# The remainder of a down projection as a fourth chunk of block products, with a rearranged end, an earlier weight split and another queue for the constants

## The chip, the core and the metric

The kernel runs on one core of one Trainium2 chip. A core has a matrix engine (TensorE, PE in the profile), a vector engine (VectorE, DVE), a scalar engine (ScalarE, ACT), a fourth general engine (GpSimd, POOL) and one that here only issues transfers (SyncE, SP). Transfers are also issued by ScalarE. Each engine works through its own list of instructions in order and waits on semaphores for the others. The metric is the device time of one execution in microseconds (us), the median of several runs.

## The reference

One encoder block on x of 1 x 1024 positions x 1024 channels, in float32; the last two steps are the ones at issue:

```python
h = rmsnorm(x, norm_mix_g[l])
z = jnp.einsum("bsd,de->bse", h, w_in[l])
... # short gated convolution; long convolution with layer norm
x = x + jnp.einsum("bse,ed->bsd", y, w_out[l])
h = rmsnorm(x, norm_ffn_g[l])
g = dwconv(jnp.einsum("bsd,df->bsf", h, w_gate[l]), conv_ffn_w[l])
v = jnp.einsum("bsd,df->bsf", h, w_up[l])
x = x + jnp.einsum("bsf,fd->bsd", jax.nn.silu(g) * v, w_down[l])
return rmsnorm(x, norm_final_g)
```

The inner width of the last part (F) is 2816, which is 22 tiles of 128. `w_down` maps these 22 tiles to 8 output tiles of 128 channels; each has 1024 positions, handled as two halves h of 512.

## The kernel before, in words

Channels lie on the 128 partitions, positions along the free axis. Every float32 product is made of three matmuls on a high and a low part of each operand (high x high, high x low, low x high), each 128 x 128 by 128 x 512. `split` makes the two parts: ScalarE copies to the high part (`whi`, `r`, `ahi`), VectorE subtracts it from the original to get the low part (`wlo`, `r`, `alo`; L93). GpSimd makes the first sums of weights (`s`, L511).

Wherever weights and operand can be cut into 2 x 2 blocks, a class `Pair` forms the product with seven block products instead of eight: m1 = A11 B11, m2 = A12 B21, m6 = S2 T2, m7 = S3 T3, m4 = A22 T4, m5 = S1 T1, m3 = S4 B22. S1 to S4 are sums of weight blocks, T1 to T4 sums of operand blocks. m1, m6, m7 and m4 accumulate in one PSUM bank (`a`), m2 in `b`, m5 and m3 in `c`; after each the running sum is taken where an output needs it. For the gate and up projections the two rows of blocks are the gate weights and the up weights of one F tile (`Ffn`, one gate/up pair per F tile); for the down projection they are two output tiles 2dp and 2dp + 1 (`Down`), and the columns are pairs of F tiles. There, half 0 of the even output tile is finished by m2, half 0 of the odd one by m4, half 1 of the odd one by m5 and m7, and half 1 of the even one by m3.

The program runs through these stages: first norm and in projection; the convolutions; out projection; second norm; gate/up, with 22 F tiles, the first ones handled apart ("plain", `NHEAD` = 2) while the operands of the block form are still being built; then the down projection. Each finished pair of F tiles 2q and 2q + 1 (pair q) goes to device memory in seven blocks (B11, T2, B21, T3, T1, T4, B22; `yd`, 256 KB each), four of which are differences made by GpSimd (L90). The down projection reads them back chunk by chunk: `NCH` = 3 chunks of `PPC` = 3 pairs, for each of four output pairs dp seven products of 3 x 3 = 9 matmuls. Two output pairs that work together are a couple. The last `NTAIL` = 4 F tiles are left over: they are stored whole (`ytail`, 512 KB each) and multiplied plainly, 12 matmuls for each of 8 tiles and 2 halves (`tail_mm`), first all of h = 0, then all of h = 1. After each, `done` adds it to the residual (VectorE), squares it (ScalarE) and adds the square to `accs[h]` (VectorE); `scale` multiplies the output by the norm's weight (ScalarE). When h = 0 is through, TensorE sums `accs[0]` over the partitions with a matrix of ones (`total3`), ScalarE takes the root (L1067), VectorE the reciprocal (L1069), and GpSimd multiplies the eight h = 0 outputs (`fin`, L1037), which SyncE stores, while TensorE works at h = 1. The last tile of h = 1 is finished in three pieces of 192, 192 and 128 positions, the multiplications shared between VectorE (5) and GpSimd (3).

TensorE's order is that of the program text (`manual_schedule`); in the last stage that of all four compute engines is. Elsewhere a scheduler sets the order of the other engines by its own costs, with `urgent` work ahead. SyncE's queue takes nearly all loads and stores in order; a store that waits for its data holds up all loads behind it.

## Time and profile before

| what | value |
|---|---|
| median of 3 runs | 1000.53 us (1000.17 to 1000.76) |
| the profiled execution, its own time | 1000.93 us |
| its span in the trace | 999.1 us |
| mean granted TensorE clock | 0.993 |
| matmul records | 4208 |
| transferred | 112.56 MB |

Times in rows of the trace count from the start of the span. A row of a timeline is: start, duration, engine, source line, operation, output <- input, shape, how many in a row, and in brackets the idle time before it and what ended it. A row of waits is: the engine and line that waited, what it waited for, us in total, how often, the longest. A row of windows is: from:to, its length, and the busy time of PE, weight load, DVE, ACT and POOL with the number of instructions, the granted clock, the busy share of the transfer engines and GB/s. A row of groups ends in count | busy us, mean ns | idle before. L93 and the like are lines of the kernel before.

### The profile page before, as it was taken

Reading aid. Unit: us, or ns where it says so; the run is one execution under the profiler, and the core shown is the slowest. Engines: PE = TensorE matmul, PEld = TensorE weight load, DVE = VectorE, ACT = ScalarE, POOL = GpSimd, SP = SyncE. Lnnn points to the kernel's source line nnn. Section 1 sums busy time; section 2 is a strip of 40 time slices with the busy share of each in tenths; the row PEclk is TensorE's granted clock in tenths of the full one; section 3 lists DMA queues with packets and bytes.
Section 4 is the critical chain, followed back from the end, with each engine's and each line's share of the span. In section 5 each row is a group of like instructions: output and inputs, shape, how many; then the busy total and the mean of one; then the engine's idle time right before and its main releaser. Section 6 shows DMA issues by size and latency. Waiting matters only on the chain.

```text
span 999.1 us, 11602 instructions
## 1 busy us (share of the span) xinstructions
PE 967.5 (97%) x4208; PEld 790.8 (79%) x4208; DVE 755.6 (76%) x888; ACT 452.8 (45%) x632; POOL 477.0 (48%) x303
## 2 busy tenths in 40 slices
...
GB/s 257 85 44 63 43 45 61 42 64 106 193 190 153 76 0 158 64 148 106 64 145 108 64 124 129 64 101 141 70 287 130 220 207 96 194 127 109 61 1 169
DMA packets 63274, 112.56 MB, mean 113 GB/s; under 512 B 5488, under 2 KB 27120, under 8 KB 62960
## 3 DMA queue, kind: packets, MB, share of 16 engines
...
q14 instruction: 25, 0.20, 0.1%
...
## 4 chain that ended last, share of the span: by engine, by line
PE 81%; DVE 9%; ACT 3%; issue 2%; DMA 1%; POOL 1%; POOLq 0%; SPq 0%; DVEq 0%; ACTq 0%
PE a L557 30%; PE mm L166 20%; PE c L557 15%; PE b L557 7%; DVE r L93 2%; PE c L692 1%; PE a L692 1%; PE mm L153 1%; PE mm L152 1%; PE mm L154 1%; PE y L154 1%; PE y L152 1%; PE y L153 1%; DMA raw<-wgate 1%; ACT whi L131 1%
## 5 line engine op out<-in xcount | busy, mean ns | idle before, releaser
L166 PE MATMUL mm<-r,whi 128*128 128x512 f32 x576 | 155.8, 389 | 0.0
L557 PE MATMUL a<-r,whi 128*128 128x512 f32 x472 | 145.7, 390 | 0.4 <-ACT a L542 0.4
L323 DVE SCALAR_TENSOR_TENSOR cv<-u,cst,cv 128x512 f32<-128x512 f32 x203 | 138.9, 751 | 1.7 <-ACT cv L317 1.2
L511 POOL TENSOR_TENSOR s<-raw,s 128x512 f32<-128x512 f32 (+1 forms) x31 | 57.5, 1854 | 161.5 <-DVE wlo L93 161.5
L166 PEld LDWEIGHTS mm<-r,whi 128*128 128x128 f32 x576 | 108.1, 188 | 22.6
L557 PE MATMUL c<-r,whi 128*128 128x512 f32 x392 | 121.1, 390 | 0.0
L93 POOL TENSOR_TENSOR wlo<-raw,whi 128x1024 fp32r<-128x1024 f32 x30 | 77.5, 2586 | 88.0 <-ACT whi L131 88.0
L131 ACT ACTIVATE whi<-raw 128x1024 fp32r<-128x1024 f32 (+1 forms) x68 | 69.2, 1020 | 103.5 <-PE mm L166 32.0
L557 PEld LDWEIGHTS a<-r,whi 128*128 128x128 f32 x472 | 88.4, 188 | 19.7 <-ACT a L542 0.8
L511 POOL TENSOR_TENSOR s<-up 128x512 f32<-128x512 f32 (+1 forms) x31 | 42.0, 1354 | 116.7 <-DMA up<-wup 96.8
L557 PE MATMUL a<-r,wlo 128*128 128x512 f32 x236 | 92.2, 391 | 2.8 <-DVE wlo L93 2.8
L166 PE MATMUL mm<-r,wlo 128*128 128x512 f32 x288 | 90.0, 389 | 0.0
L557 PEld LDWEIGHTS c<-r,whi 128*128 128x128 f32 x392 | 73.8, 188 | 16.0
L542 ACT ACTIVATE a<-a 128x512 f32<-128x512 f32 x80 | 47.5, 595 | 66.9 <-PE a L557 64.2
L131 ACT ACTIVATE whi<-s 128x1024 fp32r<-128x1024 f32 (+1 forms) x52 | 52.5, 1010 | 53.5 <-PE c L557 39.8
L557 PE MATMUL c<-r,wlo 128*128 128x512 f32 x196 | 76.5, 390 | 0.0
L635 DVE TENSOR_TENSOR t<-a,c 128x512 f32<-128x512 f32 x40 | 27.5, 687 | 64.4 <-ACT a L542 38.1
L557 PE MATMUL a<-r,ahi 128*128 128x512 f32 x224 | 70.5, 396 | 1.4 <-ACT a L542 1.4
L557 PE MATMUL b<-r,whi 128*128 128x512 f32 x232 | 71.4, 389 | 0.0
L93 DVE TENSOR_TENSOR wlo<-s,whi 128x1024 fp32r<-128x1024 f32 (+1 forms) x52 | 64.2, 1236 | 5.8 <-ACT whi L131 5.7
L131 ACT ACTIVATE r<-r 128x512 fp32r<-128x512 f32 x71 | 43.8, 628 | 49.8 <-DMA r<-ydB 23.3
L166 PEld LDWEIGHTS mm<-r,wlo 128*128 128x128 f32 x288 | 54.1, 188 | 11.2
(214 smaller groups left out, 2142.0 us busy)
## 6 DMA issues: line engine op xcount, KB each, us to landing
...
```

The lines of the kernel that those rows point to most:

```text
L93: eng.tensor_tensor(out=out, in0=a, in1=b, op=ALU.subtract)
L131: nc.scalar.activation(hi, y, AF.Copy)
L152: nc.tensor.matmul(out, whi, hi, start=first, stop=False)
L153: nc.tensor.matmul(out, whi, lo, start=False, stop=False)
L154: nc.tensor.matmul(out, wlo, hi, start=False, stop=last)
L166: nc.tensor.matmul(outs[h], w, a[h][z], start=s0, stop=s1)
L323: nc.vector.scalar_tensor_tensor(fin if k == KC - 1 else acc, src, w, acc, ALU.mult, ALU.add)
L511: self.eng.tensor_tensor(out=self.t[:, i * self.w : (i + 1) * self.w], in0=a, in1=b, op=op)
L542: nc.scalar.activation(t, b, AF.Copy)
L557: nc.tensor.matmul(out, w[wz][:, k, :], x[xz], start=first and k + wz + xz == 0, stop=k == n - 1 and wz == 1, skip_group_check=not first)
L635: nc.vector.tensor_tensor(out=out, in0=a, in1=b, op=op)
L692: nc.tensor.matmul(out, w[wz][:, k, :], xz, start=first and k == 0 and wz == 0 and xz is hi, stop=not first and k == 3 and wz == 1)
```

## The change

Four things change together.

The tail becomes a fourth chunk of the block form, with `NPL` = 2 pairs (9 and 10): 6 matmuls per product, seven products, four output pairs. The four left-over F tiles go to `yd` like the others: per pair three blocks straight and four differences from GpSimd. The last chunk's order is its own: m1, m6, m2, m7 and m4 of all four output pairs come first (m5 of the first two lies among them), so that h = 0 is complete; then the total of h = 0, now two accumulated products with ones since the last square does not go through `accs[0]`; then m5 and m3 for h = 1. In the last stage the additions of squares of h = 1 are on GpSimd (five, ahead of its eight multiplications), and VectorE multiplies all eight outputs of the first two pieces. An additional activation (Sqrt on one column, `warm`) is written before the last two m4 products. In SyncE's queue the store of the last h = 0 output pair stands behind two piece stores, with eight piece stores behind it.

In chunk 0, the sum after m5 of the first two output pairs goes through a ScalarE copy and a GpSimd addition instead of a VectorE addition.

The gate weights of F tile 3 (the fourth gate/up pair) are loaded and split before the second sums of F tile 2, into a place that the third pair's weights leave.

The constants are loaded as the first transfer of SyncE's queue instead of the first of ScalarE's.

```diff
-NTAIL = NF - 2 * NCH * PPC
+NPL = NF // 2 - NCH * PPC
...
     cuts = ((0, 2), (2, 4), (4, 8))
+    nc.sync.dma_start(cst, consts)
     nc.sync.dma_start(xs[0][:, 0, :], xT[0, :, 0])
-    nc.scalar.dma_start(cst, consts)
     load_w01(*cuts[0])
...
-    yd = {o: dpool.tile([P, NCH * PPC, H], F32, name=f"yd{o}") for o in OPS}
-    ytail = dpool.tile([NTAIL, P, S], F32, name="ytail")
+    yd = {o: dpool.tile([P, NF // 2, H], F32, name=f"yd{o}") for o in OPS}
...
-        if f >= NF - NTAIL:
-            nc.sync.dma_start(ytail[f - (NF - NTAIL)], cc)
-            return
...
-    def ff_prep(f):
-        raw, hl = g_job(f)
+    def ff_prep(f, job=None):
+        raw, hl = job or g_job(f)
...
         with urgent():
             to_op("T2", 0, 0)
+        job = g_job(NHEAD + 1)
         p2.w.update(s2.second(g2[0], up2))
         plain[1].second_b()
...
-            ff_prep(f + 1)
+            ff_prep(f + 1, job if f == NHEAD else None)
...
+    def count(ch):
+        return PPC if ch < NCH else NPL
...
         def after5(self):
-            self.add(1, 1, self.c)
+            if self.early:
+                self.add_copy(1, 1, copy_of(self.c, "c5"))
+            else:
...
     couples = [[Down(ch, 2 * i + e) for e in range(2)] for ch in range(NCH) for i in range(2)]
+    fin4 = [Down(NCH, dp) for dp in range(2)]
+    fin4 += [Down(NCH, 2 + e, rblocks[28 + 2 * e : 30 + 2 * e], rblocks[32 + 2 * e : 34 + 2 * e]) for e in range(2)]
+    couples.append(fin4[:2])
...
-        for i, pair in enumerate(couples):
+        for i, pair in enumerate(couples[:-1]):
             ch = pair[0].ch
-            reload = i % 2 and ch + 1 < NCH
+            reload = i % 2
...
-    def tail_prep(dp):
-        hl = hilo()
-        for e in range(2):
-            d = 2 * dp + e
-            raw = wraw.tile([P, NTAIL * P], F32, tag="raw", name="rawt")
-            nc.sync.dma_start(raw.rearrange("p (f m) -> p f m", m=P), wdown[d, :, NF - NTAIL :])
-            a = e * NTAIL * P
-            sl = [t[:, a : a + NTAIL * P] for t in hl]
-            split(raw, *sl, nc.vector)
-            tw[d] = parts(sl, 0, NTAIL)
-
-    def tail_mm(b, d, h):
-        for i in range(NTAIL):
-            mm3(b, tw[d][0][:, i, :], tw[d][1][:, i, :], yblock(h, i, 0), yblock(h, i, 1), i == 0, i == NTAIL - 1)
-
-    load_tail(0)
-    tail_prep(0)
-    b0 = []
-    with tc.manual_schedule(engines={nc.tensor.engine}):
-        for d in range(2):
-            b0.append(bank("y"))
-            tail_mm(b0[d], d, 0)
-        for p in couples[-1]:
-            p.m3()
-    load_tail(1)
-    rf = rup.tile([P, S], F32, tag="up", name="rf")
...
+    tq = open_pool("tq", 1)
+    accs = [tq.tile([P, H], F32, name=f"acc3{h}") for h in range(2)]
+    rf = None
 
     def scr(name):
         return cpy.tile([P, H], F32, tag="c", name=name)
 
-    acc3 = wsum.tile([P, S], F32, tag="s", name="acc")
-    accs = [half(acc3, h) for h in range(2)]
-
-    def total3(a):
+    def total3(*a):
         m = bank2("total")
-        nc.tensor.matmul(m, ones, a, start=True, stop=True)
+        for i, x in enumerate(a):
+            nc.tensor.matmul(m, ones, x, start=i == 0, stop=i == len(a) - 1)
         return m
 
     def scale(d, h):
         x = half(xf[d], h)
         nc.scalar.activation(x, x, AF.Copy, scale=col(G_FIN + d))
 
-    def done(b, d, h):
+    def final(d, h, eng=nc.vector, first=0, alone=None):
         x = half(xf[d], h)
-        nc.vector.tensor_tensor(out=x, in0=b, in1=x, op=ALU.add)
-        sq = scr("sq") if d else accs[h]
+        sq = scr("sq") if d != first else accs[h]
         nc.scalar.activation(sq, x, AF.Square)
-        if d and (h, d) != (1, KD - 2):
-            nc.vector.tensor_tensor(out=accs[h], in0=accs[h], in1=sq, op=ALU.add)
+        if d not in (first, alone):
+            eng.tensor_tensor(out=accs[h], in0=accs[h], in1=sq, op=ALU.add)
+        scale(d, h)
         return sq
 
     def fin(d, h, a, b, eng, r=None):
@@ -1045,35 +1017,71 @@
         src = (xd0, None, *xdr)[dp][:, :, cols]
         nc.sync.dma_start(outT[2 * dp : 2 * dp + 2, :, cols].rearrange("k p t -> p k t"), src)
 
+    a4, b4, c4, d4 = fin4
     with tc.manual_schedule(engines={nc.tensor.engine}):
-        for d in range(KD):
-            if d >= 2:
-                if d % 2 == 0:
-                    tail_prep(d // 2)
-                b0.append(bank("y"))
-                tail_mm(b0[d], d, 0)
-            done(b0[d], d, 0)
-            scale(d, 0)
+        for p in (a4, b4):
+            p.m1()
+        for p in couples[-2]:
+            p.m3()
+        load_op(NCH, "B22")
+        for p in (a4, b4):
+            p.prep3()
+        for p in (a4, b4):
+            p.m6()
+        for p in (c4, d4):
+            p.prep1()
+        for p in (a4, b4):
+            p.m2()
+            final(2 * p.dp, 0)
+        for p in (c4, d4):
+            p.prep2()
+            p.prep3()
+        for p in (a4, b4):
+            p.m7()
+        for p in (c4, d4):
+            p.m1()
+        for p in (a4, b4):
+            p.m4()
+            final(2 * p.dp + 1, 0)
+        for p in (c4, d4):
+            p.m6()
+        for p in (c4, d4):
+            p.m2()
+            final(2 * p.dp, 0)
+        for p in (c4, d4):
+            p.m7()
+        nc.scalar.activation(warm, eps_r, AF.Sqrt)
+        c4.m4()
+        final(5, 0)
+        d4.m4()
+        s7 = final(7, 0, alone=7)
+    rf = rup.tile([P, S], F32, tag="up", name="rf")
     with tc.manual_schedule(engines={e.engine for e in (nc.tensor, nc.vector, nc.scalar, nc.gpsimd)}):
-        for d in range(KD - 1):
-            b = bank("y")
-            tail_mm(b, d, 1)
-            if d == 1:
-                m0 = total3(accs[0])
-            s6 = done(b, d, 1)
-            scale(d, 1)
-            if d == 1:
-                std = scr("std")
-                nc.scalar.activation(std, m0, AF.Sqrt, bias=eps_r, scale=1.0 / D)
-            if d == 2:
-                nc.vector.reciprocal(rf[:, :H], std)
-                for dd in range(KD):
-                    fin(dd, 0, 0, H, nc.gpsimd)
-                    if dd % 2:
-                        store(dd // 2, 0, 0, H)
-        last = bank("y")
-        tail_mm(last, KD - 1, 1)
-        x = half(xf[KD - 1], 1)
+        a4.m5()
+        b4.m5()
+        m0 = total3(accs[0], s7)
+        std = scr("std")
+        nc.scalar.activation(std, m0, AF.Sqrt, bias=eps_r, scale=1.0 / D)
+        final(1, 1, first=1)
+        final(3, 1, nc.gpsimd, 1)
+        nc.vector.reciprocal(rf[:, :H], std)
+        c4.m5()
+        final(5, 1, nc.gpsimd, 1)
+        d4.m5()
+        final(7, 1, nc.gpsimd, 1)
+        a4.m3()
+        final(0, 1, nc.gpsimd, 1)
+        b4.m3()
+        final(2, 1, nc.gpsimd, 1)
+        for dd in range(KD):
+            fin(dd, 0, 0, H, nc.gpsimd)
+            if dd % 2:
+                store(dd // 2, 0, 0, H)
+        c4.m3()
+        s6 = final(4, 1, first=1, alone=4)
+        d4.mul(d4.c, "S4", "B22", False)
+        last = d4.c
+        x = half(xf[KD - 2], 1)
         sq, std = scr("sq"), scr("std")
         ms = []
         for a, b in PIECES:
@@ -1084,18 +1092,18 @@
             nc.tensor.matmul(m[:, a:b], ones, s6[:, a:b], start=False, stop=False)
             nc.tensor.matmul(m[:, a:b], ones, sq[:, a:b], start=False, stop=True)
             ms.append(m)
-        for (a, b), m in zip(PIECES, ms):
+        for (a, b), m, n in zip(PIECES, ms, (KD, KD, 5)):
             nc.scalar.activation(std[:, a:b], m[:, a:b], AF.Sqrt, bias=eps_r, scale=1.0 / D)
             if a == 0:
-                scale(KD - 1, 1)
+                scale(KD - 2, 1)
             rp = bank2("rp")[:, a:b]
             nc.vector.reciprocal(rp, std[:, a:b])
             nc.scalar.activation(rf[:, H + a : H + b], rp, AF.Copy)
             for d in range(KD):
-                fin(d, 1, a, b, *((nc.vector, rp) if d < 5 else (nc.gpsimd,)))
+                fin(d, 1, a, b, *((nc.vector, rp) if d < n else (nc.gpsimd,)))
                 if d % 2:
                     store(d // 2, 1, a, b)
```

Three places where the order of instructions moves. First VectorE's list at the head of the gate/up loop. Here `raw` is the gate weights of a pair, `up` its up weights, `s` sums of weights, `t` the gate values on their way through the short convolution. Before:

```order
L93 TENSOR_TENSOR xt_2613<-c,xt_2613 128x512 x2
L93 TENSOR_TENSOR wlo<-up,whi 128x512
L511 TENSOR_TENSOR s<-raw,s 128x512
L511 TENSOR_TENSOR s<-raw,up 128x512
L611 SCALAR_TENSOR_TENSOR t<-t,cst 128x1023
L612 SCALAR_TENSOR_TENSOR t<-t,cst 128x1023
L93 TENSOR_TENSOR wlo<-s,whi 128x1024
L93 TENSOR_TENSOR wlo<-raw,whi 128x1024
```

With the change:

```order
L93 TENSOR_TENSOR xt_2612<-c,xt_2612 128x512 x2
L93 TENSOR_TENSOR wlo<-raw,whi 128x1024
L93 TENSOR_TENSOR wlo<-up,whi 128x512
L510 TENSOR_TENSOR s<-raw,s 128x512
L510 TENSOR_TENSOR s<-raw,up 128x512
L610 SCALAR_TENSOR_TENSOR t<-t,cst 128x1023
L611 SCALAR_TENSOR_TENSOR t<-t,cst 128x1023
L93 TENSOR_TENSOR wlo<-s,whi 128x1024
```

The subtraction `wlo<-raw` of F tile 3 has moved from behind the two taps (L611, L612) and the subtraction of sums to the place directly behind the operands `xt`.

Second SyncE's queue where pair 9 (F tiles 18 and 19) is stored and the first operands and weights of the down projection are read. Before:

```order
L831 DMA raw<-wdown 128x3x128 x2
L831 DMA up<-wdown 128x3x128 x2
L616 DMA ytail<-t 128x1024
L831 DMA up<-wdown 128x3x128 x2
L931 DMA xd_5487<-x2d 128x1024 x2
L935 DMA xd_5486<-x2d 128x1024
L820 DMA r_94<-ydB_1793 128x512
L820 DMA r_94<-ydT_1794 128x512
L820 DMA r_94<-ydB_1793 128x512
```

With the change:

```order
L831 DMA raw<-wdown 128x3x128 x2
L831 DMA up<-wdown 128x3x128 x2
L623 DMA ydB_1793<-t 128x512
L623 DMA ydB_1797<-t 128x512
L623 DMA ydT_1792<-t 128x512
L831 DMA up<-wdown 128x3x128 x2
L623 DMA ydT_1794<-t 128x512
L939 DMA xd_5497<-x2d 128x1024 x2
L623 DMA ydT_1796<-t 128x512
L943 DMA xd_5496<-x2d 128x1024
L819 DMA r_94<-ydB_1793 128x512 x2
```

The one store `ytail` has become five stores among the loads (with two more of the same pair earlier), the last of them directly ahead of the last residual load and of the operands `r_94`.

Third GpSimd's list at the end: the last additions of sums to outputs, and the multiplications by the reciprocal root of h = 0 (128x512) and of the pieces. Before:

```order
L90 TENSOR_TENSOR xr_5700<-xr_5700,a_6833 128x512
L90 TENSOR_TENSOR xr_5701<-xr_5701,a_6846 128x512
L1037 TENSOR_TENSOR xd_5487<-xd_5487,rf 128x512 x2
L1037 TENSOR_TENSOR xd_5486<-xd_5486,rf 128x512
L1037 TENSOR_TENSOR xd_5699<-xd_5699,rf 128x512
L1037 TENSOR_TENSOR xr_5700<-xr_5700,rf 128x512 x2
L1037 TENSOR_TENSOR xr_5701<-xr_5701,rf 128x512 x2
L1037 TENSOR_TENSOR xr_5700<-xr_5700,rf 128x192
```

With the change:

```order
L90 TENSOR_TENSOR xr_5721<-xr_5721,a_7257 128x512
L90 TENSOR_TENSOR xr_5722<-xr_5722,a_7267 128x512
L1003 TENSOR_TENSOR acc_7089<-acc_7089,sq 128x512 x5
L1009 TENSOR_TENSOR xd_5497<-xd_5497,rf 128x512 x2
L1009 TENSOR_TENSOR xd_5496<-xd_5496,rf 128x512
L1009 TENSOR_TENSOR xd_5720<-xd_5720,rf 128x512
L1009 TENSOR_TENSOR xr_5721<-xr_5721,rf 128x512 x2
L1009 TENSOR_TENSOR xr_5722<-xr_5722,rf 128x512 x2
```

Between the last additions to outputs and the eight multiplications now stand five additions of squares.

50 lines of the change are left out of this document (23 added, 27 removed).

## The prediction

> **What bounds the kernel now.** I read the page first, then the busy time by stretches, then what TensorE waits for, then the rows of the places that the change touches.
>
> ```profile
> PE 967.5 (97%) x4208; PEld 790.8 (79%) x4208; DVE 755.6 (76%) x888; ACT 452.8 (45%) x632; POOL 477.0 (48%) x303
> ...
> 350.00:420.00 70.00, 66.40 (x289) 53.56 (x288) 60.81 (x65) 39.36 (x57) 27.19 (x16) 1.00 0.22 79
> 420.00:725.00 305.00, 305.00 (x1340) 251.23 (x1339) 179.20 (x160) 130.71 (x160) 157.95 (x95) 1.00 0.30 103
> 725.00:780.00 55.00, 50.50 (x211) 40.25 (x211) 45.96 (x47) 31.88 (x51) 32.05 (x18) 0.97 0.62 198
> 780.00:900.00 120.00, 118.15 (x518) 96.73 (x517) 101.23 (x127) 53.77 (x84) 57.25 (x43) 1.00 0.55 171
> 900.00:940.00 40.00, 40.00 (x177) 32.90 (x176) 26.65 (x39) 15.58 (x25) 6.89 (x6) 1.00 0.34 106
> ```
>
> TensorE is the bound: busy for 967.5 of 999.1 us, and in the gate/up loop (420 to 725) for all of 305.00 us with 1340 matmuls, so one matmul costs 305.00 / 1340 = 0.2276 us there. What is left to win without fewer matmuls stands in three stretches: 3.6 us before 420, 4.5 us in 725 to 780, 1.85 us in 780 to 900. The waits name what ends last in them:
>
> ```profile
> PE a L557 <- DVE r L93: 3.4, 2, 2.8
> PE a L557 <- DVE wlo L93: 2.8, 3, 1.8
> PE mm L274 <- DVE whi L246: 1.9, 1, 1.9
> PE a L557 <- DVE xd L863: 1.9, 2, 1.4
> PE mm L274 <- DVE r L214: 1.8, 2, 1.1
> PE a L557 <- ACT a L542: 1.8, 2, 1.4
> ```
>
> All are VectorE or ScalarE work that TensorE catches up with. At the end the order is another one: the last products are followed by a chain of small operations and stores.
>
> **The matmuls and the end.** The tail of 8 x 2 x 12 = 192 matmuls becomes a chunk of 4 x 7 x 6 = 168: 24 x 0.2276 = 5.46 us less. These rows carry the rest:
>
> ```profile
> 965.12 1.02 PE L1019 MATMUL total<-acc,ones_r 128*128 128x512 f32 x2
> 965.58 0.79 PE L152 MATMUL y<-r,whi 128*128 128x512 f32 x1
> 982.08 0.39 PE L154 MATMUL y<-r,wlo 128*128 128x512 f32 x1
> ...
> 967.45 1.28 ACT L1067 ACT_TABLE_LOAD   x1
> 968.75 0.69 ACT L1067 ACTIVATE std<-total,eps_r 128x512 f32<-128x512 f32 x1
> 969.64 0.63 ACT L1030 ACTIVATE sq<-xd 128x512 f32<-128x512 f32 x1 [0.20 <-DVE xd L1028]
> 970.30 0.73 ACT L1024 ACTIVATE xd<-xd,cst 128x512 f32<-128x512 f32 x1
> ...
> 968.91 0.69 DVE L1028 TENSOR_TENSOR xd<-y,xd 128x512 f32<-128x512 f32 x1 [1.51 <-PE y L154]
> 970.91 3.35 DVE L1069 RECIPROCAL rf<-std 128x512 f32<-128x512 f32 x1
> 977.55 1.66 DVE L1032 TENSOR_TENSOR acc<-acc,sq 128x512 f32<-128x512 f32 x1 [0.70 <-ACT sq L1030]
> ...
> 974.40 5.95 POOL L1037 TENSOR_TENSOR xd<-xd,rf 128x512 f32<-128x512 f32 x4 [63.03 <-DVE rf L1069]
> 980.32 5.66 POOL L1037 TENSOR_TENSOR xr<-xr,rf 128x512 f32<-128x512 f32 x4
> L1037 POOL TENSOR_TENSOR xd<-xd,rf x4: 1290/1514/1753, 974.4 to 978.6; 128x512 f32<-128x512 f32 x4
> 994.84 0.94 SPq L1043 DMA_DIRECT2D outT<-xd  x2
> 996.36 0.42 SPq L1046 DMA_DIRECT2D outT<-xr  x1
> ```
>
> A sum over partitions with the matrix of ones is two records 0.43 apart (965.12 to 965.98, where the next matmul would stand); the h=0 total now has two terms, so +0.86. It also comes sooner behind its input. Its first term needs output 5, which the last-but-one product before it finishes: VectorE adds it (0.69), ScalarE squares it (0.63), VectorE adds output 7 meanwhile and then the square (0.69), which together puts the total 2.9 us behind that product, and TensorE has only one product of 6 x 0.2276 = 1.37 us to run: +1.5 us of stall. The last product therefore ends 5.46 - 0.86 - 1.5 = 3.1 us earlier: at 979.2 instead of 982.3 on the time scale of before.
>
> That gain does not reach the end of the span, because the path changes. Behind the total stand 36 matmuls (8.2 us), so it ends at 971.0; the root (0.69) at 971.9, the reciprocal (3.35) at 975.3. VectorE is behind that reciprocal with its first m5 sum (to 976.0). Then ScalarE needs 0.63 + 0.73 + 0.03 = 1.39 us for square and scaling of each of the four outputs 5, 7, 0 and 2, so the last square of these is there at 976.0 + 3 x 1.39 + 0.63 = 980.8, and GpSimd, which now adds the squares, is done at 980.8 + 1.3 = 982.1. In front of GpSimd's eight h=0 multiplications stand five such additions, where in before the first multiplication started at 974.40 and the last ended at 985.98. At the fast end of their row (1290 ns) eight take 10.3 us: 992.4. SyncE's queue, in order, holds the store of the last h=0 outputs and eight piece stores behind it, issued 0.48 apart (0.94 and a gap for two): the last at 992.4 + 8 x 0.48 = 996.2 instead of 996.36, and what follows an issue stays. Term: **-0.1**. Below, it is -3.1 if GpSimd were out of the way; above, +3.7 if all eight cost 1753 ns. I take 1290 because the slow ones of before ran beside VectorE's additions of squares (977.55, 1.66 instead of 0.69), and these are no longer there.
>
> [...]
>
> The additional square-root activation does not shorten this: the order has it among ScalarE's first instructions, so the table load (1.28) stays in front of the root, where it ends about 0.2 us after the total. It costs nothing measurable at either place (0 to 0.2).
>
> **The fourth gate/up pair's weights.** The waits for wlo and for ScalarE's copy stand between 379 and 412:
>
> ```profile
> 378.58 1.23 DVE L93 TENSOR_TENSOR wlo<-s,whi 128x1024 fp32r<-128x1024 f32 x1 [0.35 <-ACT whi L131]
> 378.87 2.07 POOL L511 TENSOR_TENSOR s<-up 128x512 f32<-128x512 f32 x1 [65.07 <-DMA up<-wup]
> 379.73 2.30 DVE L93 TENSOR_TENSOR wlo<-raw,whi 128x1024 fp32r<-128x1024 f32 x1
> 382.08 0.50 PE L557 MATMUL a<-r,wlo 128*128 128x512 f32 x1 [1.79 <-DVE wlo L93]
> ...
> 395.49 0.69 DVE L635 TENSOR_TENSOR t<-a,b 128x512 f32<-128x512 f32 x1 [4.14 <-POOL t L90]
> 403.59 2.31 DVE L611 SCALAR_TENSOR_TENSOR t<-t,cst 128x1023 f32<-128x1023 f32 x1
> 405.94 2.20 DVE L612 SCALAR_TENSOR_TENSOR t<-t,cst 128x1023 f32<-128x1023 f32 x1
> 408.23 1.06 ACT L613 ACTIVATE t<-t 128x1024 f32<-128x1024 f32 x1 [4.19 <-DVE t L612]
> 410.14 1.06 ACT L542 ACTIVATE a<-a 128x512 f32<-128x512 f32 x2
> ```
>
> At 382.08 TensorE has waited for the 2.30 us subtraction of the pair's low parts, which started only at 379.73. In the new order it stands before the third pair's sums, at about 373, where GpSimd is idle and it takes 1.23. That removes 1.79 and the 0.2 before it: 2.1 us with the gaps between matmuls. TensorE then reaches the next places 2.1 earlier. Whether the smaller waits there come back is decided by VectorE: it idles 4.14 us until 395.49 behind GpSimd, and that GpSimd chain itself starts with VectorE products that move about 1.9 earlier. The next pair's wlo (the row of 2.8 in three leaves 1.0 for two other waits; half of it here) now stands ahead of the wait for GpSimd, so this one goes too. At 411.2 (1.4) the copy follows the silu at 408.23, which follows the two taps at 403.59 and 405.94; these move some 2.1 earlier, but one more split now stands between the two copies (1.04). So 2.1 is sure, and 4.2 (with 0.5 and 1.6) the most. I take **-2.6**, nearer to the lower end. Without the cover, the wait only moves to 401 or 411, and the term is about 0.
>
> **The hand-over to the down projection, 725 to 780.**
>
> ```profile
> 735.00:747.00 12.00, 12.00 (x54) 9.94 (x53) 4.70 (x6) 2.43 (x5) 5.89 (x4) 1.00 0.93 323
> 771.00:780.00 9.00, 6.01 (x18) 4.56 (x19) 9.00 (x8) 2.78 (x4) 8.66 (x5) 0.81 0.34 110
> 736.44 1.65 POOL L511 TENSOR_TENSOR s<-up 128x384 f32<-128x384 f32 x1 [6.79 <-DMA up<-wdown]
> L90 POOL TENSOR_TENSOR xd<-xd,a 128x512 f32<-128x512 f32 x4 | 9.1, 2272 | 9.1 <-ACT a L542 9.1
> ```
>
> From 735 to 747 the DMA engines are 0.93 busy at 323 GB/s, and VectorE works only 4.70 of 12 us since it waits for operands. Pair 9 used to put one 512 KB store per tile there; now come seven stores of 256 KB, of which five stand in SyncE's queue in this stretch, the last behind GpSimd's four differences, all ahead of the chunk-0 operands. More data: 0.78 MB / 0.323 = 2.4 us; the queue: about 2 us, mostly the same time. VectorE is busy 9.00 of 9.00 in 771 to 780, so what it starts later it ends later, and TensorE (wait for r, 2.8) pays. Some of it the idle VectorE time after 747 covers: **+1.5**, from 0 to +3.5.
>
> **Couples of chunk 0, 780 to 900.** VectorE hands two additions (0.68 to 1.8) to ScalarE and GpSimd before the wait for xd (1.4), which can vanish; against it, pair 10's four differences now load GpSimd (8.66 of 9.00 busy after 771), and the outputs arrive behind more stores, which VectorE's idle time in that stretch (120 - 101.23) covers: **-0.7**, from -2.2 to +2.
>
> **Chunk 4's operands and weights.** VectorE splits them from 900 on, where it is busy 26.65 of 40 us, so the cover is there: **+0.3**, to +2.5 if a wait per couple remains.
>
> **Start.** The constants and the first weights change places as first transfers, a wait of 1.9 (whi) against one of 1.8 (r): what one gains of its 0.45 us issue the other loses, and ScalarE's two weight casts move ahead of four activations: **0**, from -1.5 to +1.
>
> **Sum:** -0.1 - 2.6 + 1.5 - 0.7 + 0.3 = **-1.6** against the profiled execution of 1000.93 us (span 999.1 and 1.8 around it). The median of the runs is 0.4 lower, 1000.53, so the forecast is **998.9 us**.
>
> **Rivals.**
> - *The end is not GpSimd's.* If ScalarE's squares come early enough that the multiplications run before the last products, the whole 3.1 arrives: 998.9 - 3.0 = 995.9. For it: GpSimd has only these 13 instructions in the last 25 us. Against it: the order of the queue and ScalarE's 1.39 per output.
> - *The removed wait reappears at 401 or 411.* 998.9 + 2.6 = 1001.5. For it: ScalarE's order there; against it: VectorE's idle 4.14.
> - *GpSimd pays the shared price at the end.* If its instructions cost 1.65 in the mean instead of 1.29, eight multiplications and some three unhidden additions cost 11 x 0.36 = 4.0 more: 1002.9, slower. It decides from a mean of 1.62 on (3.6 over the forecast). For it: the 1753 of before; against it: fewer VectorE additions.
> - *The operands of chunk 0 wait for GpSimd.* If its four differences cost 2272 ns each as the row of additions there does, they end 9.1 after the product instead of 5.2, SyncE's loads stand 3.9 longer, and TensorE's wait grows by that: 998.9 + 3.9 = 1002.8, slower. It decides from 3.6 us more on. For it: saturated DMA and a VectorE at 9.00 of 9.00; against it: GpSimd has idled 6.79 us by 736.44.
> - *The square root's warming up does nothing*, as the order shows: in the sum already.
>
> **How the numbers follow.** A measurement of this kernel can tell about 0.2%, 2.0 us, from no change: 998.5 and 1002.5 are the borders. Chances: the forecast 0.37 (its own range 996.9 to 1000.9, a little less than half of it below the border), the end free of GpSimd 0.26, the wait that reappears 0.10, GpSimd's shared price 0.09, the late operands 0.10, and 0.08 for sums of smaller misses on either side. Faster: 0.17 + 0.26 + 0.03 = 0.46; within 0.2%: 0.20 + 0.10 + 0.03 = 0.33; slower: 0.09 + 0.10 + 0.02 = 0.21. The range of 8 in 10 takes in the free end with half a spread below it and the slower cases up to their price: 994.3 to 1003.0.
>
> **What would show it.** Matmuls: 24 fewer of the products. End: the last GpSimd multiplication of h=0 near 992, later than 985.98 was, and SyncE's store of it directly in front of the last eight. Head: no wait for wlo near 380, and one for ScalarE's copy near 409. Hand-over: a longer wait for r after 770. Wrong would be a GpSimd row that ends before 988, a wait for r that shrinks, or a wait for wlo that stays.

## The result, and the profile after

The changed kernel takes **1007.28 us** (median of 4 runs, 1006.23 to 1007.78) where the kernel before takes 1000.35 in the same comparison: a ratio of 1.0069 with a 95% interval of 1.0057 to 1.0081. It is slower by 6.9 us; the forecast was 998.9 with a range up to 1003.0. The profiled execution is the fastest of the four, 1006.23 us with a span of 1004.1, against 1000.93 and 999.1 before. So the two traces have 5.0 us of span to explain; the rest of the 6.9 lies in where these two executions stand among the runs of their kernels.

First the page's line of busy times, of the kernel after:

```profile
PE 967.7 (96%) x4186; PEld 789.4 (79%) x4186; DVE 768.0 (76%) x908; ACT 461.0 (46%) x653; POOL 516.8 (51%) x332
```

22 matmul records fewer (24 products less, two more for the total), and yet TensorE is busy as long as before: 0.2 us more. GpSimd carries 40 us more. The same stretches as before, kernel after:

```profile
350.00:420.00 70.00, 67.75 (x291) 55.28 (x290) 57.77 (x66) 40.12 (x57) 28.68 (x16) 0.98 0.22 79
420.00:725.00 305.00, 305.00 (x1340) 251.30 (x1339) 180.10 (x160) 130.71 (x160) 159.10 (x96) 1.00 0.30 103
725.00:780.00 55.00, 50.88 (x214) 40.51 (x213) 49.57 (x47) 31.57 (x51) 36.02 (x21) 0.97 0.67 214
780.00:900.00 120.00, 114.71 (x499) 93.07 (x498) 98.52 (x121) 52.91 (x84) 67.75 (x49) 1.00 0.56 179
900.00:940.00 40.00, 40.00 (x177) 32.91 (x176) 29.65 (x43) 17.48 (x29) 14.88 (x15) 1.00 0.42 126
```

Three readings. From 350 to 420 TensorE gains two matmuls only (291 instead of 289), with a granted clock of 0.98. From 780 to 900 it does 19 matmuls fewer (499 instead of 518, 19 x 0.2276 = 4.3 us), at full clock: it waits. And it is VectorE that worked *less* there (98.52 instead of 101.23) while GpSimd worked 10.5 us more. The waits of TensorE in the whole span, kernel after:

```profile
PE a L556 <- DVE r L93: 3.4, 2, 2.8
PE a L556 <- ACT whi L131: 3.2, 1, 3.2
PE total L1091 <- POOL acc L1003: 2.7, 1, 2.7
PE a L556 <- ACT a L541: 2.2, 1, 2.2
PE a L556 <- DVE xr L865: 1.9, 1, 1.9
...
PE a L556 <- DVE wlo L93: 0.7, 1, 0.7
```

The wait for wlo in the head is gone; the 0.7 that is left of 2.8 lies in the hand-over, where the kernel before has it too. The one for ScalarE's copy has become one of 2.2. The wait for r is unchanged (3.4, longest 2.8). Two are new in the chunks, for ScalarE's whi (3.2) and for VectorE's xr (1.9), and one at the end, for GpSimd's sum of squares (2.7).

Where the position of TensorE in its own list stands against before, by instruction: at 378: +0.2. At 428, behind the head: -0.2. At 772, behind the hand-over: -0.5. At 847: +4.0. At 900: +3.7. At the last product: +0.9. At the end of the span: +5.0. By terms of the sum:

| term | forecast | measured |
|---|---|---|
| start, and all up to 378 | 0 | +0.2 |
| head (fourth pair's weights) | -2.6 | -0.4 |
| hand-over, 725 to 780 | +1.5 | -0.3 |
| couples of chunk 0 and the next, 780 to 900 | -0.7 | +4.2 |
| chunk 4's operands | +0.3 | 0.0 |
| end | -0.1 | +1.3 |
| sum | -1.6 | +5.0 |

**The stretch 780 to 900.** SyncE's queue in the kernel before, then after:

```profile
783.87 0.34 SPq L616 DMA_DIRECT2D ytail<-t  x1
784.30 0.38 SPq L907 DMA_DIRECT2D xd<-x2d  x1
...
788.37 1.01 SPq L831 DMA_DIRECT2D raw<-wdown  x2
```

```profile
783.64 0.80 SPq L623 DMA_DIRECT2D ydB<-t  x2
786.48 3.86 SPq L623 DMA_DIRECT2D ydT<-t  x3
790.51 0.32 SPq L915 DMA_DIRECT2D xd<-x2d  x1
...
793.53 0.38 SPq L831 DMA_DIRECT2D raw<-wdown  x1
```

The residual loads (`x2d`) start 6.2 us later, behind the last three difference stores of pair 10 (F tiles 20 and 21), and the weight loads (`wdown`) 5.2 us later. GpSimd's list in the same place, before and after:

```profile
785.38 1.67 POOL L511 TENSOR_TENSOR s<-raw,s 128x384 f32<-128x384 f32 x1 [2.63 <-DVE wlo L93]
787.01 1.33 POOL L511 TENSOR_TENSOR s<-raw,up 128x384 f32<-128x384 f32 x1
```

```profile
784.45 5.54 POOL L90 TENSOR_TENSOR t<-t 128x512 f32<-128x512 f32 x3
...
791.51 1.02 POOL L510 TENSOR_TENSOR s<-raw,s 128x384 f32<-128x384 f32 x1
792.48 1.02 POOL L510 TENSOR_TENSOR s<-raw,up 128x384 f32<-128x384 f32 x1
```

Before, GpSimd has idled 2.63 us when the sums of weights can start at 785.38; the second ends at 788.34, and the weight load into the place that it has read is issued at 788.37. After, three of pair 10's differences and an addition lie there; the second sum ends at 793.50, and the load is issued at 793.53. VectorE, in order, then stands at the late residual (kernel after):

```profile
795.05 0.69 DVE L865 TENSOR_TENSOR xd<-xd,a 128x512 f32<-128x512 f32 x1 [4.64 <-DMA xd<-x2d]
```

Before, the same addition starts 5.7 us earlier:

```profile
789.37 0.69 DVE L863 TENSOR_TENSOR xd<-xd,a 128x512 f32<-128x512 f32 x1 [1.91 <-DMA xd<-x2d]
```

So GpSimd's four differences (2.27 us for the first, at 776.58, and 5.54 for the three above: 7.8) make two kinds of transfers late at once. From 784 to 792 the transfer engines move much less than before, first before, then after:

```profile
784.00:792.00 8.00, 8.00 (x37) 6.50 (x35) 4.92 (x8) 2.22 (x4) 6.62 (x6) 1.00 0.92 323
```

```profile
784.00:792.00 8.00, 8.00 (x37) 6.52 (x36) 6.32 (x5) 3.14 (x6) 8.00 (x6) 1.00 0.55 178
```

What was not moved then is still moving later (a share of 1.12 from 800 to 808, where before has 0.72), and the operands of chunk 1 (`r<-ydB`, `r<-ydT`) come among it: the first three are issued from 794.02 on, before from 795.59, but land a median of 8.3 us after their issue instead of 5.0. ScalarE splits them when they land, before and after:

```profile
800.63 1.95 ACT L131 ACTIVATE r<-r 128x512 fp32r<-128x512 f32 x3 [3.65 <-DMA r<-ydB]
```

```profile
801.42 0.63 ACT L131 ACTIVATE r<-r 128x512 fp32r<-128x512 f32 x1 [4.99 <-DMA r<-ydB]
803.88 1.34 ACT L131 ACTIVATE r<-r 128x512 fp32r<-128x512 f32 x2 [1.82 <-DMA r<-ydB]
```

VectorE has made up most of the late residual by 799.41 (before stands there at 798.32), then waits for these splits, three times and 5.1 us between 800 and 810 (before once, 2.3). So its addition of `a` to `xr`, which releases the bank that TensorE wants, starts at 813.50 instead of 810.89. TensorE waits at 814.23 (2.05 us) for this and at 838.56 (3.37, where before had 1.58) for ScalarE's late `whi`.

**The head.** ScalarE's list, kernel after:

```profile
407.95 1.06 ACT L131 ACTIVATE whi<-s 128x1024 fp32r<-128x1024 f32 x1 [3.19 <-POOL s L510]
408.91 0.58 ACT L541 ACTIVATE a<-a 128x512 f32<-128x512 f32 x1
```

The copy of F tile 3's accumulator after m7 stands behind the weight split `whi<-s`, and that one waits for GpSimd's sum until 407.95. TensorE waits 2.35 us at 409.55 and then runs at half clock for some time. The windows show it, first the kernel after, then a kernel with the same wait (2.34 us at 409.27, the run b_job below) in which the clock stays:

```profile
409.00:413.00 4.00, 3.46 (x10) 2.74 (x11) 3.96 (x4) 1.44 (x3) 1.67 (x2) 0.68 0.71 260
```

```profile
409.00:412.00 3.00, 2.73 (x12) 2.23 (x13) 3.00 (x4) 1.17 (x2) 1.05 (x1) 1.00 0.86 330
```

The granted clock is 0.68 against 1.00: some eight matmuls follow each other at a pitch of 0.43 instead of 0.23 us, which costs 1.5 us.

**The end.** GpSimd's and SyncE's lists, kernel after:

```profile
980.88 5.36 POOL L1003 TENSOR_TENSOR acc<-acc,sq 128x512 f32<-128x512 f32 x4 [1.57 <-ACT sq L1001]
986.20 5.11 POOL L1009 TENSOR_TENSOR xd<-xd,rf 128x512 f32<-128x512 f32 x4
991.27 4.93 POOL L1009 TENSOR_TENSOR xr<-xr,rf 128x512 f32<-128x512 f32 x4
```

```profile
996.45 0.46 SPq L1018 DMA_DIRECT2D outT<-xr  x1
997.00 0.44 SPq L1015 DMA_DIRECT2D outT<-xd  x1
997.54 1.60 SPq L1018 DMA_DIRECT2D outT<-xr  x2
...
1000.82 0.93 SPq L1018 DMA_DIRECT2D outT<-xr  x2
```

The last addition ends at 986.24, the eighth multiplication at 996.20, and the last h = 0 store goes at 996.45 with eight piece stores behind it, the last at about 1001.3. From the last product (983.4) to the end of the span stand 20.7 us, where before had 16.6.

### The profile page after: what moved, and what is told of

It is laid out like the page before. It is cut to its first block, busy times and chain, and to the rows that moved or that the text cites. A ratio compares the mean times of both kernels' runs of the same rounds, so it can differ in the third digit from the quotient of the medians.

```text
span 1004.1 us, 11721 instructions
## 1 busy us (share of the span) xinstructions
PE 967.7 (96%) x4186; PEld 789.4 (79%) x4186; DVE 768.0 (76%) x908; ACT 461.0 (46%) x653; POOL 516.8 (51%) x332
## 5 line engine op out<-in xcount | busy, mean ns | idle before, releaser
L556 PE MATMUL a<-r,whi 128*128 128x512 f32 x496 | 153.2, 390 | 0.0
L510 POOL TENSOR_TENSOR s<-raw,s 128x512 f32<-128x512 f32 (+2 forms) x35 | 61.1, 1745 | 167.3 <-DVE wlo L93 166.7
L131 ACT ACTIVATE whi<-raw 128x1024 fp32r<-128x1024 f32 (+2 forms) x72 | 71.6, 997 | 104.8 <-PE b L556 32.5
L556 PEld LDWEIGHTS a<-r,whi 128*128 128x128 f32 x496 | 93.0, 188 | 20.0 <-ACT a L541 0.4
L510 POOL TENSOR_TENSOR s<-up 128x512 f32<-128x512 f32 (+2 forms) x35 | 46.9, 1342 | 118.6 <-DVE wlo L93 67.0
L556 PE MATMUL a<-r,ahi 128*128 128x512 f32 x240 | 76.9, 402 | 4.1 <-ACT a L541 2.2
L131 ACT ACTIVATE whi<-s 128x1024 fp32r<-128x1024 f32 (+2 forms) x54 | 53.8, 996 | 57.1 <-PE c L556 38.3
L90 POOL TENSOR_TENSOR t<-t 128x512 f32<-128x512 f32 x44 | 70.4, 1612 | 18.2 <-DVE t L613 18.2
L631 DVE TENSOR_TENSOR t<-a,c 128x512 f32<-128x512 f32 x40 | 27.4, 686 | 65.7 <-ACT a L541 38.1
L556 PE MATMUL b<-r,whi 128*128 128x512 f32 x248 | 76.4, 389 | 0.0
L93 DVE TENSOR_TENSOR wlo<-s,whi 128x1024 fp32r<-128x1024 f32 (+2 forms) x54 | 65.8, 1218 | 11.7 <-ACT whi L131 11.5
```

The lines of the kernel that those rows point to most:

```text
L90: nc.gpsimd.tensor_tensor(out=out, in0=a, in1=b, op=op)
L93: eng.tensor_tensor(out=out, in0=a, in1=b, op=ALU.subtract)
L131: nc.scalar.activation(hi, y, AF.Copy)
L510: self.eng.tensor_tensor(out=self.t[:, i * self.w : (i + 1) * self.w], in0=a, in1=b, op=op)
L556: nc.tensor.matmul(out, w[wz][:, k, :], x[xz], start=first and k + wz + xz == 0, stop=k == n - 1 and wz == 1, skip_group_check=not first)
L631: nc.vector.tensor_tensor(out=out, in0=a, in1=b, op=op)
```

## The experiments

The comparisons below have the kernel before beside them, at 1000.2 to 1000.5 us. `[...]` is the 95% interval of the ratio to it. Where an expectation speaks of the weight loads of "the second couple" near 790, they are by SyncE's list those of the third couple, the first of chunk 1. Several kernels here leave a part of the computation out, as each text says; they show what that part costs, and are no replacement.

**dve_adds: the end's additions of squares on VectorE.**

```diff
-        final(1, 1, first=1)
-        final(3, 1, nc.gpsimd, 1)
         nc.vector.reciprocal(rf[:, :H], std)
+        final(1, 1, first=1)
         c4.m5()
-        final(5, 1, nc.gpsimd, 1)
+        final(3, 1, nc.vector, 1)
...
```

> The changed kernel with the five additions of h=1 squares back on VectorE, one output later than their sums so that it does not wait for ScalarE; the reciprocal stands ahead of them. Theory A, GpSimd's thirteen instructions set the end: its eight multiplications start at the reciprocal (979.6 in the trace of the change) instead of 986.2, and the end falls back on the last product plus some 16.7 us as before, 983.4 + 16.7 = 1000.1 of span instead of 1004.1, so about 1003.3 us instead of 1007.3. Theory B, the end follows the last product and the pieces: no change, 1007.3 within 0.7.

Measured: 1010.56 us, 1.0095 [1.0074, 1.0117]. Slower still by 3.3; both theories missed. In 978 to 988 VectorE is busy 10.00 of 10.00. Its additions of squares, and GpSimd's multiplications beside them:

```profile
981.77 1.46 DVE L1003 TENSOR_TENSOR acc<-acc,sq 128x512 f32<-128x512 f32 x1
983.15 0.67 DVE L865 TENSOR_TENSOR xr<-xr,c 128x512 f32<-128x512 f32 x1
983.75 1.18 DVE L1003 TENSOR_TENSOR acc<-acc,sq 128x512 f32<-128x512 f32 x1
```

```profile
981.38 6.36 POOL L1009 TENSOR_TENSOR xd<-xd,rf 128x512 f32<-128x512 f32 x4 [20.07 <-DVE rf L1065]
987.71 6.07 POOL L1009 TENSOR_TENSOR xr<-xr,rf 128x512 f32<-128x512 f32 x4
```

Freed of the additions, GpSimd starts at 981.38 instead of 986.20, but a multiplication then costs 1.55 instead of 1.25, and an addition on VectorE 1.15 to 1.46 instead of the 0.68 of the kernel after. VectorE gets to the last tile late and becomes the bound of the end. The choice of GpSimd was the better of the two; what it costs is another run's question (no_h1_adds).

**c5_dve: the sum after m5 of the early couple back on VectorE.**

```diff
         def after5(self):
-            if self.early:
-                self.add_copy(1, 1, copy_of(self.c, "c5"))
-            else:
-                self.add(1, 1, self.c)
+            self.add(1, 1, self.c)
```

> The changed kernel with the sum after m5 of the first two output pairs of chunk 0 back on VectorE (two ScalarE copies and two GpSimd additions less). Theory A, SyncE's queue is held by pair 10's stores, which wait for GpSimd's differences: the loads of the second couple come at most 1 us earlier, 1006.5 to 1007.3, and the waits at 814 and 838 stay over 4 us together. Theory B, the additional copies and additions themselves make the second couple late: both waits shrink to the 1.6 of before together, 1003 to 1004.

Measured: 1006.71 us, 1.0055 [1.0036, 1.0075]. The waits at 814 and 838 are gone, and in their place stands one of 4.91 us at 797.75, where TensorE wants a bank that VectorE has not read, being held up at the late residual load. The time is theory A's, the waits are neither's: the loss moved. So these two additions are not its cause.

**nodiff10, nodiff10_c5, diff10_dve: pair 10's differences.** The first leaves them out, the second leaves them out and has the sum after m5 on VectorE, the third makes them on VectorE.

```diff
+        if f == NF - 1:
+            for o, t, h in (("B11", ye, 0), ("B21", yo, 0), ("T1", ye, 0), ("T2", ye, 1), ("T3", yo, 0), ("T4", ye, 1), ("B22", yo, 1)):
+                nc.sync.dma_start(yd[o][:, f // 2, :], half(t, h))
+            return
```

```diff
-        pool(half(t12, 0), half(ye, 1), half(ye, 0), ALU.subtract)
...
+        def dif(out, x, y, op):
+            (nc.vector if f == NF - 1 else nc.gpsimd).tensor_tensor(out=out, in0=x, in1=y, op=op)
+
+        dif(half(t12, 0), half(ye, 1), half(ye, 0), ALU.subtract)
...
```

> The changed kernel without GpSimd's four differences for pair 10; its seven stores stay and send undifferenced halves (this part of the computation is left out). Theory A, SyncE's queue held by these differences: the residual loads start near 785 instead of 790.5, the second couple's weights too, and TensorE's waits at 814 and 838 (5.4 us) fall to about 1.6 as before: 1003.0 to 1003.8. Theory B, the additional bytes of the seven stores or the ScalarE copies make it late: not more than 1 us is won, 1006.3 to 1007.3.

> The changed kernel without pair 10's differences (undifferenced halves are stored, as in the run that left them out) and with the sum after m5 of the first two output pairs back on VectorE. Theory A: with the differences out of SyncE's queue the residual loads are early enough for VectorE, so no wait near 798 appears, and the waits at 814 and 836 (2.0 and 2.2 without the differences alone) fall to one of about 1.6 as in before: 2 to 2.7 us less than 1003.5, so 1000.8 to 1001.5. Theory B: the late loads come from the number of stores, and the wait near 798 of 4.9 comes back: 1003 to 1005.

> The changed kernel with pair 10's four differences on VectorE instead of GpSimd. Theory A, what counts is that SyncE waits for GpSimd: four VectorE operations (2.8 us at 0.69) replace four of GpSimd (7.6 us), the last store goes out about 4 us earlier, and as much is won as without the differences less VectorE's 2.8: 1004.0 to 1006.0. Theory B, VectorE, busy all of 771 to 780, is what counts: the wait for r at 776 and the later ones grow, 1007.5 to 1010.

Measured: nodiff10 1003.53 us, 1.0033 [1.0021, 1.0045]; nodiff10_c5 1003.79, 1.0034 [1.0021, 1.0047]; diff10_dve 1006.30, 1.0059 [1.0040, 1.0079]. The four differences are worth 3.7 us of the median, more than half of the whole loss, and with them gone it makes no difference where the sum after m5 is done. Theory A of nodiff10 has the time right, but not the waits. The residual loads start at 784.86 and the weight loads at 789.12, almost as in the kernel before, and from 784 to 792 the transfers run at 330 GB/s again, but TensorE's waits do not fall to 1.6 (nodiff10, TensorE from 800 to 842, then VectorE):

```profile
PE a L556 <- DVE xr L870: 2.4, 2, 1.9
PE a L556 <- DVE xd L870: 2.1, 1, 2.1
```

```profile
802.32 0.69 DVE L93 TENSOR_TENSOR r<-r 128x512 fp32r<-128x512 f32 x1 [5.27 <-ACT r L131]
```

VectorE waits 5.27 us for ScalarE's split, and ScalarE 6.65 for `r<-ydB` to land: the operands of chunk 1 are still late (the first split starts at 801.65, in the kernel after at 801.42, before at 800.63), with no difference in the way. nodiff10_c5 keeps the same two waits (2.1 and 1.9, and none near 798), so its theory A, 1000.8 to 1001.5, is missed. Made on VectorE the differences cost almost as much as on GpSimd (-1.0 from the kernel after, between the two theories, the intervals overlapping): the residual loads still start only at 790.1.

**stores3: also without four of the seven stores.** Chunk 4 reads pair 9's differences instead. Against nodiff10:

```diff
-            for o, t, h in (("B11", ye, 0), ("B21", yo, 0), ("T1", ye, 0), ("T2", ye, 1), ("T3", yo, 0), ("T4", ye, 1), ("B22", yo, 1)):
+            for o, t, h in (("B11", ye, 0), ("B21", yo, 0), ("B22", yo, 1)):
```

> The changed kernel without pair 10's four differences and with only its three straight blocks stored; chunk 4 reads pair 9's differences in place of pair 10's, so a part of the output is computed from other data (left out: the differences of the last pair). Nothing else is changed, the loads of chunk 4 are as many as before. Theory A (the amount of stores ahead of the residual and weight loads holds SyncE's queue, beside the differences themselves): the first residual load, which stood at 784.9 without the differences alone, is issued before 783, the first weight load of the second couple before 788, the wait near 813 (2.0 without the differences) falls below 1.2, and the span lies 1 to 2 us below the 1001.8 without the differences: 1001.5 to 1002.8 us. Theory B (only the wait for the differences held the queue; the waits that are left are the scheduler's order of VectorE and ScalarE): wait near 813 stays at 2.0 +-0.3, time 1003.5 +-0.5.

Measured: 1003.07 us, 1.0028 [1.0017, 1.0040]. In its profiled execution (999.2 span) the residual loads start at 783.03, the weight loads at 787.11, and of TensorE's waits from 800 to 842 one of 0.3 is left:

```profile
PE a L556 <- DVE xd L870: 0.3, 1, 0.3
```

So in that execution theory A holds and more; but the median, 0.3 above theory A's range, is only 0.5 below nodiff10's, and the two intervals overlap. Of the 2.6 us between the two profiled spans, 1.5 are the half clock behind the wait near 409, which nodiff10 had and this execution did not. What the four stores themselves cost stays open.

TensorE's own stretch from 428 to 900, read from the starts of the same products and compared with the kernel before, puts these runs side by side. It is 3.9 us longer in the kernel after, and 4.9 to 6.5 in the four profiled kernels that have the same program up to there (no_h1_adds, no_h1_adds_5, h0_poolq, dve_adds). Without the differences it is 2.5 and 2.0 longer, without the four stores too 0.3. The granted clock in the hand-over differs between these executions (1.00 from 773 to 781 in nodiff10, 0.57 in stores3), so the shares are rough; but a part of the loss stays when the differences go.

**no_h1_adds, no_h1_adds_5: the end without GpSimd's five additions,** and then also with the pieces shared 5 to 3 between VectorE and GpSimd, as in the kernel before.

```diff
-        if d not in (first, alone):
+        if d not in (first, alone) and not h:
```

```diff
-        for (a, b), m, n in zip(PIECES, ms, (KD, KD, 5)):
+        for (a, b), m, n in zip(PIECES, ms, (5, 5, 5)):
```

> The changed kernel without the five GpSimd additions of h=1 squares (the sum of squares of h=1 then lacks five of its eight terms). Theory A, GpSimd's thirteen instructions set the end through SyncE's queue: the multiplications start at 979.6 and end near 990, TensorE's wait of 2.9 in front of the last total goes, and the end is that of the pieces, 3 to 4 us earlier: 1003.3 to 1004.3. Theory B, the pieces set it already: at most the 2.9 of TensorE's wait is visible and less than 1 us arrives at the end, 1006.3 to 1007.3.

> The changed kernel without GpSimd's five additions of squares of h=1 (left out: their part of the last norm), and with the pieces' multiplications shared 5 to 3 between VectorE and GpSimd in all three pieces, as in the kernel before. Theory A (VectorE's eight multiplications a piece set the pitch of the pieces, 3.86 instead of 3.08): the end comes 1.2 to 1.8 us sooner than with the additions alone left out, the stretch from the h=0 total to the end 26.6 to 27.1 instead of 28.3, time 1002.6 to 1003.3. Theory B (GpSimd's h=0 multiplications, which then have the three of each piece behind them, end no sooner, or the pieces wait for GpSimd): 28.3 +-0.4, time 1004.0 to 1004.9.

Measured: 1004.45 us, 1.0037 [1.0024, 1.0049], and 1003.02, 1.0033 [1.0021, 1.0046]. From the start of the h = 0 total to the end of the span: 30.7 us in the kernel after (973.38 to 1004.1), 28.3 without the additions, 27.4 with the pieces shared as well. So GpSimd's five additions cost 2.4 there, a little less than the 3 to 4 of theory A, and all eight multiplications on VectorE another 0.9; theory A of the second run had the time right and the stretch 0.3 to 0.8 too short.

**h0_poolq: the h = 0 stores issued by GpSimd instead of SyncE.**

```diff
+        q = nc.sync if h else nc.gpsimd
...
-                nc.sync.dma_start(outT[d, :, cols], xf[d][:, cols])
+                q.dma_start(outT[d, :, cols], xf[d][:, cols])
```

> The changed kernel with the five stores of h=0 issued by GpSimd behind its own multiplications instead of by SyncE. Theory A, the place of the last h=0 store in SyncE's queue sets the end: without it the last piece store goes out at about 998.6 + 5 x 0.5 at most, and with the earlier piece stores out of the way 1 to 2 us are won, 1005.3 to 1006.3. Theory B, the pieces or GpSimd's own time (issuing costs it time between its multiplications) set it: 1007 to 1009.

Measured: 1008.95 us, 1.0083 [1.0065, 1.0102], theory B's range. The issue is not free where GpSimd is the chain: 0.57 to 0.87 us each, between the multiplications, and the last of these ends at 998.5 instead of 996.2.

**b_job, b_job_v, b_cst: parts of the change on the kernel before.** b_job has the early split of F tile 3's weights alone. b_job_v has in addition the copy of F tile 3's accumulator after m7 on VectorE. b_cst has the constants on SyncE's queue alone.

```diff
+        job = g_job(NHEAD + 1)
         p2.w.update(s2.second(g2[0], up2))
...
-            ff_prep(f + 1)
+            ff_prep(f + 1, job if f == NHEAD else None)
```

```diff
-            self.a2 = copy_of(self.a, "a2")
+            if self.f == NHEAD + 1:
+                self.a2 = cpy.tile([P, H], F32, tag="c", name="a2")
+                nc.vector.tensor_copy(self.a2, self.a)
+            else:
+                self.a2 = copy_of(self.a, "a2")
```

> The kernel before with only the earlier load and split of F tile 3's gate weights. Theory A, as the trace of the change shows it: the waits at 382 and 401 go, the one at 411 grows from 1.6 to 2.4 and is followed by some matmuls at half clock, so 0.3 to 0.9 us are won, 999.5 to 1000.1. Theory B, the forecast: 2.6 won, 997.8.

> The kernel before with the early split of F tile 3's weights only (999.10 us measured), and the copy of F tile 3's accumulator after m7 taken by VectorE instead of ScalarE, where it stood behind a weight split and let TensorE wait 2.34 us at 409.27. Theory A (the gain of the head is eaten by the place of this copy in ScalarE's list, and by the matmuls at half clock behind the wait): the wait near 409 falls below 0.6, no half-clock matmuls follow, span 2 to 3.5 us below 996.6: 993.1 to 994.6, time 995.5 to 997. Theory B (VectorE is as late as ScalarE there, or the wait returns at the next product): a wait of 1.5 us or more between 405 and 425 stays, time 998.3 to 999.4.

> The kernel before with one line moved: the constants are the first transfer of SyncE's queue instead of the first of ScalarE's. Theory A (what one queue gains the other loses, as forecast): TensorE's first product within 0.2 us of 7.11, time 1000.4 +-0.5. Theory B (the first operand comes later by a whole transfer): first product 0.5 to 1.0 later, time 1000.9 to 1001.5.

Measured: b_job **999.10** us, 0.9984 [0.9975, 0.9994]; b_job_v **996.74**, 0.9965 [0.9951, 0.9978]; b_cst 1000.08, 0.9997 [0.9989, 1.0006]. The early split gains 1.4 us by itself, between the two theories, and 3.5 with the copy moved. In b_job_v VectorE, which idles there, does the copy in time:

```profile
404.93 0.68 DVE L650 COPY a<-a 128x512 f32<-128x512 f32 x1
408.55 1.22 DVE L93 TENSOR_TENSOR wlo<-s,whi 128x1024 fp32r<-128x1024 f32 x1 [2.94 <-ACT whi L131]
```

The wait of 2.34 is gone; one of 0.97 follows at the next bank. b_job_v is faster than both kernels of this case. The constants' queue makes no difference to the median, as forecast, though TensorE's first product comes 0.4 us sooner in the trace, not within the 0.2 of theory A.

**p10_poolq, after_v, p10_poolq_v: the whole changed kernel, with one or two things moved.** The first has GpSimd issue pair 10's four difference stores, so that SyncE's queue waits for none of them; the second has F tile 3's copy on VectorE; the third has both.

```diff
-            nc.sync.dma_start(yd[o][:, f // 2, :], half(t, h))
+            q = nc.gpsimd if f == NF - 1 and o[0] == "T" else nc.sync
+            q.dma_start(yd[o][:, f // 2, :], half(t, h))
```

> The changed kernel, complete, with one thing moved: the stores of pair 10's four differences are issued by GpSimd, which makes the differences, instead of by SyncE. Theory A (SyncE's queue waits for these differences, and the residual and weight loads of the second couple stand behind it): without them in the queue the first weight load of the second couple is issued before 788 (793.5 with the change), the waits at 814 (2.05) and 838 (3.37) together lose at least 2.5, GpSimd pays four issues of some 0.6: span 2 to 3.5 us below 1004.1, time 1003.5 to 1005.3. Theory B (the amount of transfers or GpSimd's own lateness makes the operands late, the queue only shows it): the two waits together stay above 4.5, time 1006.5 to 1008.5.

> The changed kernel, complete, with the copy of F tile 3's accumulator after m7 taken by VectorE instead of ScalarE. Theory A (the wait that the early weight split leaves at 409.55 is only the place of this copy behind the weight split in ScalarE's list): the wait falls from 2.35 to 1.0 or less, the matmuls behind it keep their full clock, time 2 to 3 us below 1007.28: 1004.3 to 1005.3. Theory B (the gain is taken back at the hand-over or in chunk 0, where TensorE then arrives earlier at operands that are no earlier): time 1006 to 1007.5.

> The two preceding edits together: pair 10's difference stores issued by GpSimd, and F tile 3's copy on VectorE. Theory A (the two losses are independent and both are mended): 4 to 6 us below 1007.28, 1001.3 to 1003.3; what stays over the kernel before with the same head (996.74) is the end, some 4 to 6 us. Theory B (an earlier TensorE waits in chunk 0 for the same operands): the gains don't add up, 1004 to 1006.

Measured: p10_poolq 1011.30 us, 1.0104 [1.0091, 1.0118]; after_v 1005.39, 1.0044 [1.0029, 1.0060]; p10_poolq_v 1008.76, 1.0086 [1.0072, 1.0099]. The copy on VectorE is worth 1.9 in one and 2.5 in the other, against 2.4 on the kernel before (b_job to b_job_v): about the same with and without the other losses, though the runs of one kernel spread by 2 to 4 us. after_v lies 0.1 above its theory A, and theory A's sum of both gains was missed, since moving the stores gained nothing. It made things worse, and the waits say why. SyncE from 783 to 796, then TensorE from 800 to 848, in p10_poolq:

```profile
SPq L832 <- POOL s L510: 9.6, 1, 9.6
```

```profile
PE a L556 <- DVE xr L866: 7.8, 2, 7.6
```

No store holds the queue now, and still the first weight load is issued only at 794.44, after 9.6 us of waiting for GpSimd's sums, which stand behind the differences:

```profile
792.43 1.03 POOL L510 TENSOR_TENSOR s<-raw,s 128x384 f32<-128x384 f32 x1
793.41 1.01 POOL L510 TENSOR_TENSOR s<-raw,up 128x384 f32<-128x384 f32 x1
```

In this kernel's list the residual loads stand behind these weight loads (802.48 instead of 790.51), and TensorE waits 7.6 us for VectorE's addition to the residual. Theory A falls: with no store in the way the first weight load goes at 794.44, not before 788, since GpSimd's list is late by the differences whoever issues their stores. What the queue's hold by the stores alone costs isn't shown by this run, since the scheduler put the residual loads elsewhere with the edit.

## Why the prediction was wrong

**The step that failed most** is the couples after 780, -0.7 forecast and +4.2 measured. The prediction saw pair 10's four differences and GpSimd at 8.66 of 9.00, and then costed them at nothing with a cover that is none: "VectorE's idle time in that stretch (120 - 101.23) covers". VectorE's idle time is not where these instructions run. They run on GpSimd, in front of its sums of weights, and the sums release the places of the next weights; the differences' stores stand in SyncE's queue in front of the residual loads, which VectorE needs in order. VectorE even idled longer than before (4.64 for x2d, then 5.1 for operands). Leaving the differences out took 3.7 us of the median (nodiff10), and p10_poolq shows the lateness of the sums with its wait of 9.6 us. The same sentence also covered the outputs' arrival "behind more stores" with VectorE's idle time, and that may have failed too: without the differences, and with the loads issued almost as early as before, waits of 1.9 and 2.1 us stayed, behind operands that landed late; only without the four stores were they gone, in one execution (stores3). Whether it is these stores that keep them there is not shown. The rival of late operands had this mechanism, but for pair 9's differences at the hand-over and with the operands of chunk 0, where nothing came of it; it was priced at 1002.8 and given 0.10. Pair 10's four differences took 7.8 us of GpSimd, where the prediction had used 5.2 for pair 9's four and nothing for these. How the loss divides between the residual loads, the weight loads and the operands behind them was not separated.

**The head**, -2.6 forecast and -0.4 measured: the rival that the removed wait reappears at 401 or 411. The wait for wlo went as worked out (2.1 us). The step that failed is that the copy "follows the silu", which moves earlier (403.22 instead of 408.23): ScalarE takes the weight split `whi<-s` between them, and this one waits for GpSimd until 407.95. The prediction did name a split between the two copies, with 1.04 us, but not that the split itself waits. b_job_v settles it on the kernel before: with that one copy on VectorE the early split's gain is 3.5, more than the forecast's 2.6; in the changed kernel the same edit gained 1.9 (after_v). A part of what is missing is chance, the half clock behind the wait (below): in b_job's profiled execution, where the clock stayed full, the head gains 2.0.

**The hand-over**, +1.5 forecast, -0.3 measured: TensorE's waits there are 0.91, 0.75 and 2.92, before 0.55, 0.87, 0.80 and 2.92. GB/s rose from 198 to 214 and the share of the transfer engines from 0.62 to 0.67, but none of TensorE's waits there grew by more than 0.04 with pair 9's stores, that for r included. The term came out just below its lower bound, 0.

**The end**, -0.1 forecast, +1.3 measured; its mechanism was right step by step. The last product was worked out 3.1 us earlier and came 2.8 earlier by its own stretch (+3.7 at 900 becomes +0.9). GpSimd's last multiplication was put at 992.4 and ended at 996.20, which less the 3.7 that TensorE brought along is 992.5, with 1.25 us per multiplication where 1.29 was taken. That this chain sets the end shows in no_h1_adds, where the stretch shrinks by 2.4. The term that was mis-sized is the row of stores behind it: eight at 0.61 instead of 0.48, which is 1.0, and 0.25 from the multiplication to its store. The rival that the end is not GpSimd's had a chance of 0.26 and found no support. The rival of GpSimd's shared price did not happen in the change: the last four multiplications, from 991.27 on, ran beside VectorE's piece multiplications (from 989.94 on) and took 4.93 us together. But dve_adds shows that such a price exists: 1.55 instead of 1.25 on GpSimd, and 1.15 to 1.46 instead of 0.68 on VectorE, when VectorE adds squares beside it; VectorE's sums from PSUM between these additions took 0.67 to 0.68, in the kernel after 0.69.

**The chances.** The forecast and all four rivals that had a time lay below 1003.0. The two mechanisms that happened, a wait that reappears (2.2 over the term) and GpSimd late at what others need (4.9 over the term), were taken as alternatives at 0.10 each, and came together; nothing in the prediction made the one exclude the other. Of the 5.5 us of 24 matmuls, 2.8 were left at the last product, and the end took them and 1.3 more; without GpSimd's additions, which the result needs, and with shared pieces it was 3.3 shorter (no_h1_adds_5).
